# Counting a 388-column weight piece as 0.76 of a step in a schedule written out by hand

## The chip, the cores and the metric

The kernel runs on one core of a Trainium2 chip. The metric is the device time of one execution in microseconds; the median of three runs is compared. One execution is also profiled, and its trace is what the text reads.

## What is computed

Two layers, each on x of 256 x 2048 with one combined input projection that feeds three kinds of heads. The output of each kind is gated by a SiLU path, and one output projection and a normalisation follow. In short:

```python
h = x @ w_in
a_q, a_k, a_v, a_z, b_q, b_k, b_v, b_z, b_lr, m_q, m_z = jnp.split(h, cuts, axis=-1)
y_a = chunk_band_attention(heads_a(a_q), heads_a(a_k), heads_a(a_v), rel_table)   # 8 heads of 128
log_g = jax.nn.log_sigmoid(b_lr @ gate_w + gate_b) / GATE_TAU
o_b = gla_chunk_recurrence(heads_k(b_q), heads_k(b_k), b_v, heads_k(log_g))       # 4 heads
o_b = o_b * lax.rsqrt(jnp.mean(jnp.square(o_b), axis=-1, keepdims=True) + RMS_EPS) * gla_norm_g
y_m = memory_attention(heads_m(m_q), heads_m(mk), heads_m(mv))                    # 4 heads, 256 memory rows
y = jnp.concatenate([y_a * silu(a_z), y_b * silu(b_z), y_m * silu(m_z)], axis=-1)
x = layer_norm(DEEPNORM_ALPHA * x + y @ w_out, ln_g, ln_b)
```

## The kernel before

**Projections.** Every projection is a stream of weight pieces. `piece` (L128) loads one piece with a DMA on SP's queue and splits it into a high part (a cast on ScalarE, L116) and a low part (a subtraction on VectorE, L117), because the products are formed from split operands; the pool holds four raw pieces and four of each part. TensorE multiplies each piece with the resident x (all through `mm`, L93). There are two shapes of stream. `ws_group` (L254) runs two halves of four pieces with 256 columns and four rows of k each; a group is 8 pieces. `as_group` (L272) runs 8 pieces of `n` columns and two rows of k; `n` is 512 for the memory values, the GLA gate and the output projection, and 388 for the four value projections, `values(0)` to `values(3)` (L797).

**The order.** The order on TensorE and on SP's queue is the program's own (L49). VectorE and ScalarE are ordered by the scheduler when the program is built, with the splits of weights at a high priority; on the chip that order is then fixed. The work that isn't projection is written as Python generators: `gla` (L311), eight `a_head`s (L503), four `m_head`s (L537), `gla_turned` (L487), and in the second layer `transposed` (L574) and `restored` (L602). A generator issues a stretch of instructions, yields the number of ticks until its next stretch, and so on. `tick` (L52) is called after each weight piece: it raises `now` by one, keeps at most two generators active, and runs at most one stretch that is due (a generator that ends hands on to the next within the same tick). So a stretch is placed on TensorE's queue behind the piece whose tick ran it, and everything that it issues, its DMAs too, goes there. `finish` (L69) ticks on until named generators are done.

**The order of a layer** is: memory keys and values; GLA's q and k (BQK); `values(0)`, `values(1)`; then `gla` is put into the queue; for each half `values(2 + half)`, the queries (AQ) and the keys (AK), then four `a_head`s into the queue (L831 to L836); the memory queries (MQ), then four `m_head`s; the GLA gate (BZ), the other gates, and the output projection. Below, V0 to V3 are the value projections, and "V3 #2" is the second piece of V3.

**What the stretches hold.** `gla` has eight, with yields of 2, 6, 2, 6, 6, 3 and 2 ticks between them. Counted from 0: 0 and 1 are the gates' logits, their sigmoid and the running sum (table functions on ScalarE); 2 turns the decayed keys on TensorE; 3 to 5 hold the decayed products in six levels, each level a subtraction, |.|, an exponential and two products (L376), matmuls (L316) and a masked copy on VectorE (L335); 6 the outputs (L451 to L471), with four PSUM banks, four copies on ScalarE (L465) and eight squares (L470); and the end is an inverse square root (L285, with Sqrt on ScalarE, L289) and two scalings (L476). An `a_head` has three, with yields of 3 and 2 ticks between them and of 2 at its end: the bias load for the head two further on (L506) and the scores with their softmax (L508 to L521), the transposes (L526) with a copy (L528), and the values (L532, L534). `restored` multiplies and adds the normalisation's rows, two VectorE operations a stretch (L607, L608), eight stretches 2 ticks apart; it is put into the queue ahead of V0 in the second layer and finished (L827) ahead of V2.

The pool of PSUM banks that the stretches use has four (L84), taken in turn.

Of the kernel before, what the change touches and what calls it, by code (L numbers as in the profile page):

```python
# [36 lines left out]
def hybrid_trunk_kernel(  # L37
# [11 lines left out]
    ctx.enter_context(tc.manual_schedule(engines={PE, mybir.EngineType.SP}))  # L49
    waiting, active, done, now = [], [], set(), [0]  # L50

    def tick():  # L52

        now[0] += 1
        while True:
            while waiting and len(active) < 2:
                active.append((waiting.pop(0), 0))
            due = [e for e in active if e[1] <= now[0]]
            if not due:
                return  # L60
            active.remove(due[0])
            g = due[0][0]
            after = next(g, None)
            if after is not None:
                active.append((g, now[0] + after))
                return
            done.add(g)

    def finish(gens):  # L69
        while not all(g in done for g in gens):  # L70
            tick()
# [16 lines left out]
    def nm(s):  # L88
        uid[0] += 1
        return f"{s}_{uid[0]}"  # L90
# [28 lines left out]
    def load_quarter(src):  # L119

        with tc.high_priority(AHEAD):
            raw = wp.tile([P, 4, T], F32, name=nm("raw"), tag="raw")
            x = operand()
            sp.dma_start(raw, src)
            parts(x[0], x[1], raw)
        return x

    def piece(src, n, kp=2, home=None):  # L128

        with tc.high_priority(AHEAD):  # L130
            raw = wp.tile([P, kp, n], F32, name=nm("raw"), tag="raw")
            if home is None:
                hi, lo = (wp.tile([P, kp, n], F32R, name=nm(w), tag=w) for w in ("wh", "wl"))
            else:
                hi, lo = home
            if isinstance(src, list):
                w = n // len(src)
                for i, part in enumerate(src):
                    sp.dma_start(raw[:, :, i * w:(i + 1) * w], part.rearrange("p (k n) -> p k n", k=kp))
            else:  # L140
                sp.dma_start(raw.rearrange("p k n -> p (k n)"), src)
            parts(hi, lo, raw)
        return hi, lo
# [96 lines left out]
    def ws_half(src, xq):  # L240

        acc = psd.tile([P, 2, 2, T], F32, name=nm("acc"), tag="acc")
        for pc in range(4):
            wh, wl = piece(src[pc], 256, 4)
            xh, _, both = xq[pc]
            for j in range(4):
                for b in range(2):
                    mm(acc[:, b].rearrange("p h t -> p (h t)"), wh[:, j, b * P:(b + 1) * P], both[:, j], pc == j == 0, False)
                for b in range(2):
                    mm(acc[:, b, 1], wl[:, j, b * P:(b + 1) * P], xh[:, j], False, pc == j == 3)  # L250
            tick()
        return acc
# [11 lines left out]
    def as_products(o, t, xq, w, kt, kk, first=0):  # L264
        wh, wl = w
        xh, xl, _ = xq[kt // 4]
        j, ts = kt % 4, slice(t * P, (t + 1) * P)
        mm(o, xh[:, j, ts], wh[:, kk], kt == first, False)
        mm(o, xl[:, j, ts], wh[:, kk], False, False)
        mm(o, xh[:, j, ts], wl[:, kk], False, kt == 15)  # L270

    def as_group(src, xq, n, kp=2, first=None):  # L272

        acc = psd.tile([P, 2, 512], F32, name=nm("acc"), tag="acc")
        for pc in range(16 // kp):
            if first is not None and pc % 2 == 0:
                xq.append(load_quarter(first[pc // 2]))
            w = piece(src[pc], n, kp)
            for kk in range(kp):
                for t in range(2):  # L280
                    as_products(acc[:, t, :n], t, xq, w, pc * kp + kk, kk)
            tick()
        return acc

    def rsqrt(dst, src, n, epsc):  # L285
# [474 lines left out]
    for l in range(L):  # L760
# [3 lines left out]
        if l == 0:  # L764
            def each(p):
                if p in (2, 4, 6, 7):
                    xq.append(resident_quarter(len(xq), xT[len(xq)]))

            first_memory(mk, mv, each)
        else:  # L770
            memq = []
            parts(*mv, as_group(w512[l, G_MV], memq, 512, 2, memT))
            gens = [transposed(xq, gbT), restored(gb)]
            waiting.append(gens[0])
            for i, a, b in ws_group(w512[l, G_MK], memq):
                tmp = scratch([P, 2, T])
                total(tmp, a, b)
                parts(mk[0][:, i:i + 2], mk[1][:, i:i + 2], tmp)
            finish(gens[:1])
# [17 lines left out]
        def values(i):  # L797
            acc = as_group(w388[l, i], xq, 388)
            act.copy(asv[:, :, i * 388:(i + 1) * 388], acc[:, :, :388])
# [38 lines left out]
        for i, a, b in ws_group(w512[l, G_MQ], xq):  # L838
# [5 lines left out]


        acc = as_group([[w512[l, G_BZ, h * 4 + pc // 2][:, pc % 2 * 512:pc % 2 * 512 + 512] for h in range(2)]
                        for pc in range(8)], xq, 512)
        finish(gens[0])
# [156 lines left out]
```

## Time and profile before

| | us |
|---|---|
| median of 3 runs | 927.55 |
| lowest and highest | 927.30, 927.62 |
| span of the profiled execution | 924.8 |
| TensorE busy in it | 917.4 |
| VectorE busy | 588.4 |
| ScalarE busy | 497.1 |
| DMA, bytes moved | 178.85 MB, 193 GB/s in the mean |

The profile gives no time of its own for the profiled execution beside its span, which runs from the first to the last instruction. The median of the runs lies 2.75 us above it, and this difference is taken for what lies around the span.

How to read its rows: PE is TensorE's matmuls, PEld its weight loads, which run beside them, DVE VectorE, ACT ScalarE, SP the queue of DMAs. A row of the waits has the waiting engine, what it was to write and its line, what it waited for, then the sum in us, how often, and the longest. A row of the chain has its start, its length, and what ran. A row of the timeline has its start, length, engine, line, operation, the tile written and those read, shapes and count, and in brackets the idle time before it with what ended it. A row of the groups has the count, then busy us, mean ns of one, and the idle time before.

### The profile page before, as it was taken

The page shows a single profiled execution, that of the slowest core. Times are in us where ns is not written, and L with a number is a line of the kernel's source. Part 1 is how long each engine was busy: PE and PEld are TensorE (multiplying, and loading weights), DVE is VectorE, ACT ScalarE, POOL GpSimd, SP SyncE. Part 2 cuts the span into 40 slices and gives each one's busy share as a digit, 9 for nine tenths or more (in the row PEclk, how much of TensorE's full clock was granted, in tenths as well). Part 3 has the DMA queues.
Part 4 walks back from the last instruction along what each step waited for, and adds up shares of the span by engine and source line. Part 5 has one row for each costly group of instructions (what it writes and reads, how often), then busy time and mean ns, then how long its engine had stood idle before and what let it go on. Part 6 is the DMA issues. An engine that isn't in the chain of part 4 may idle for free.

```text
span 924.8 us, 14242 instructions
## 1 busy us (share of the span) xinstructions
PE 917.4 (99%) x5500; PEld 807.1 (87%) x5500; DVE 588.4 (64%) x812; ACT 497.1 (54%) x714; POOL 21.9 (2%) x49
## 2 busy tenths in 40 slices
PE   9999999999999999999999999999999999999997
PEld 8889998998888888888888899889888888888885
DVE  6764488564564666555587674975646555766565
ACT  6644475574454675433466446656544555754350
POOL 1000000000000000000000000000000000110000
PEclk9999999999999999999999999999999999999999
DMA  9956865555555566766675566565555544676652
GB/s 310 332 187 176 303 208 158 167 191 172 187 160 161 172 202 206 214 193 196 213 252 175 151 205 190 182 184 166 189 185 176 166 152 160 197 223 221 200 163 91
DMA packets 71253, 178.85 MB, mean 193 GB/s; under 512 B 7304, under 2 KB 31240, under 8 KB 70928
## 3 DMA queue, kind: packets, MB, share of 16 engines
q1 hardware_dynamic: 69120, 173.30, 58.4%
q0 software_dynamic: 1920, 4.36, 2.0%
q8 instruction: 43, 0.70, 0.3%
q10 hardware_dynamic: 144, 0.26, 0.1%
q14 instruction: 26, 0.21, 0.1%
HBM read 175.77 MB, written 2.10 MB: 192 GB/s over the span
## 4 chain that ended last, share of the span: by engine, by line
PE 95%; ACT 2%; issue 1%; DVE 1%; DMA 0%; SPq 0%; DVEq 0%; ACTq 0%
PE acc L93 86%; PE bk L93 7%; ACT wh L116 1%; PE bk L526 1%; ACT sc L470 1%; DMA raw<-w 0%; PE bk L561 0%; PE bk L590 0%; ACT L518 0%; ACT L289 0%; ACT yr L465 0%; PE bk L494 0%; DVE yr L476 0%; ACT sc L518 0%; ACT sc L528 0%
## 5 line engine op out<-in xcount | busy, mean ns | idle before, releaser
L117 DVE TENSOR_TENSOR wl<-raw,wh 128x1024 fp32r<-128x1024 f32 (+3 forms) x321 | 369.9, 1154 | 252.6 <-ACT wh L116 250.1
L116 ACT CAST wh<-raw 128x1024 fp32r<-128x1024 f32 (+3 forms) x321 | 318.4, 994 | 327.3 <-PE acc L93 229.7
L93 PE MATMUL acc<-x,wh 128*128 128x512 f32 x1248 | 397.6, 400 | 0.1
L93 PE MATMUL acc<-wh,x 128*128 128x512 f32 (+2 forms) x1236 | 358.1, 371 | 0.0
L93 PEld LDWEIGHTS acc<-x,wl 128*128 128x128 f32 x1248 | 234.4, 188 | 55.3
L93 PEld LDWEIGHTS acc<-wh,x 128*128 128x128 f32 x1236 | 227.5, 189 | 27.6 <-issue 0.3
L93 PE MATMUL acc<-x,wl 128*128 128x256 f32 x1248 | 246.0, 278 | 0.0
L93 PE MATMUL acc<-wl,x 128*128 128x512 f32 (+2 forms) x618 | 228.1, 369 | 0.0
L93 PEld LDWEIGHTS acc<-x,wh 128*128 128x128 f32 x1248 | 191.8, 189 | 1.8 <-ACT wh L116 0.3
L93 PEld LDWEIGHTS acc<-wl,x 128*128 128x128 f32 x618 | 116.2, 188 | 14.5 <-DVE wl L117 0.6
L518 ACT ACTIVATE sc<-sc,mx 128x128 f32<-128x128 f32 (+1 forms) x32 | 14.4, 449 | 21.8 <-DVE mx L516 21.8
L382 ACT ACTIVATE sc<-sc 128x512 f32<-128x512 f32 x12 | 7.6, 633 | 18.4 <-DVE sc L380 18.4
L511 DVE SCALAR_TENSOR_TENSOR sc<-bk,bias 128x384 f32<-128x384 f32 x16 | 8.9, 556 | 12.3 <-PE bk L93 12.2
L117 DVE TENSOR_TENSOR x<-sc,x 128x512 fp32r<-128x512 f32 x20 | 13.3, 684 | 0.7 <-ACT x L116 0.7
L116 ACT CAST x<-raw 128x1024 fp32r<-128x1024 f32 x5 | 5.3, 1052 | 15.0 <-DMA raw<-memT 12.6
L117 DVE TENSOR_TENSOR x<-raw,x 128x1024 fp32r<-128x1024 f32 x5 | 6.1, 1220 | 11.0 <-ACT x L116 11.0
L93 PE MATMUL bk<-qk,qk 128*128 128x128 f32 (+1 forms) x64 | 13.1, 326 | 0.0
L93 PE MATMUL bk<-sc,asv 128*128 128x256 f32 (+1 forms) x64 | 13.0, 326 | 0.0
L262 DVE SCALAR_TENSOR_TENSOR sc<-acc,sc 128x512 f32<-128x512 f32 x19 | 12.9, 681 | 0.0
L117 DVE TENSOR_TENSOR x<-res,x 128x512 fp32r<-128x512 f32 (+2 forms) x14 | 10.4, 764 | 3.9 <-ACT x L116 3.9
L623 DVE SCALAR_TENSOR_TENSOR res<-res,acc 128x512 f32<-128x512 f32 x15 | 9.7, 683 | 5.0 <-PE acc L93 5.0
L116 ACT CAST x<-sc 128x512 fp32r<-128x512 f32 x20 | 11.8, 615 | 1.3 <-DVE sc L598 1.3
(209 smaller groups left out, 568.4 us busy)
## 6 DMA issues: line engine op xcount, KB each, us to landing
raw<-w SPq DMA_DIRECT2D x214, 512.0 KB, 4.0
raw<-w SPq DMA_DIRECT2D x64, 388.0 KB, 3.4
raw<-w SPq DMA_DIRECT2D x83, 256.0 KB, 3.2
bias<-relw SPq DMA_DIRECT2D x16, 192.0 KB, 3.8
res<-xT SPq DMA_DIRECT2D x4, 512.0 KB, 4.9
res<-xn SPq DMA_DIRECT2D x1, 2048.0 KB, 8.2
raw<-memT SPq DMA_DIRECT2D x4, 512.0 KB, 4.2
res<-memT SPq DMA_DIRECT2D x6, 256.0 KB, 6.2
```

The costliest lines, as they stand in the source:

```text
L93: pe.matmul(o, l, r, start=start, stop=stop, skip_group_check=True)
L116: act.copy(hi, src)
L117: dve.tensor_tensor(lo, src, hi.bitcast(F32), op=ALU.subtract)
L262: dve.scalar_tensor_tensor(dst, a, scale, dst, op0=ALU.mult, op1=ALU.add)
L382: act.activation(dd, dd, AF.Abs)
L470: act.activation(sq, on[par][:, g], AF.Square, scale=1.0 / math.sqrt(P), accum_out=ms[:, par * 4 + g:par * 4 + g + 1])
L511: dve.scalar_tensor_tensor(s, pb[:, :384], SCALE, bias[h], op0=ALU.mult, op1=ALU.add)
L518: act.activation(s[:, own[t]], s[:, own[t]], AF.Exp, bias=mx[:, t:t + 1], accum_out=zs[:, t:t + 1])
L526: pe.transpose(pt[:, i * P:(i + 1) * P], s[:, i * P:(i + 1) * P], ident)
L623: dve.scalar_tensor_tensor(r, r, ALPHA, acc, op0=ALU.mult, op1=ALU.add)
```

## The change

`tick` takes a share, 1 unless given, and raises `now` by it. `as_group` passes its columns over 512. So a piece of 388 columns counts 388/512 = 0.7578; the pieces of 512 columns and those of `ws_group` count 1 as before. The yields stay as they are.

```diff
-    def tick():
+    def tick(share=1.0):
 
-        now[0] += 1
+        now[0] += share
...
             for kk in range(kp):
                 for t in range(2):
                     as_products(acc[:, t, :n], t, xq, w, pc * kp + kk, kk)
-            tick()
+            tick(n / 512)
         return acc
```

## The prediction

> **What bounds the kernel now.** I read the page first, then who TensorE's two queues wait for, then the stretches in which the moved steps lie, and last the order of work inside them.
>
> ```profile
> span 924.8 us, 14242 instructions
> PE 917.4 (99%) x5500; PEld 807.1 (87%) x5500; DVE 588.4 (64%) x812; ACT 497.1 (54%) x714; POOL 21.9 (2%) x49
> PEclk9999999999999999999999999999999999999999
> ```
>
> TensorE is busy for 917.4 of 924.8 us at full granted clock. A busy share alone can hide waits, so the next view asks for them: first the matmuls' waits, all of them, then the weight loads' waits that bear on this change.
>
> ```profile
> PE bk L93 <- DVE eps L759: 1.1, 1, 1.1
> PE bk L526 <- DVE sc L521: 0.5, 2, 0.3
> PE bk L93 <- ACT nparts L116: 0.3, 1, 0.3
> PE bk L734 <- DVE nt L696: 0.3, 1, 0.3
> ```
>
> ```profile
> PEld bk L526 <- DVE sc L521: 1.2, 2, 0.6
> PEld bk L93 <- DVE mx L516: 0.5, 2, 0.2
> ```
>
> The first row is the start of the program; the last two (tiles of the closing normalisation) are its end. Between them the matmuls wait in one place per layer: L526, the transposes of an attention head, for L521, the last operation of that head's softmax. It costs 0.5 us in all (0.27 each by the rows below). That is what the change can win; with the weight loads' waits at the same places the bound is 1.2 + 0.5 = 1.7 us.
>
> The place is found in the stretches by group of weight pieces. In order: the fourth value projection (V3) of layer 0, the query projection behind it (AQ1), the memory-query projection (MQ), and V3 of layer 1.
>
> ```profile
> 173.96:195.57 21.61, 21.34 (x168) 20.41 (x167) 14.12 (x29) 18.36 (x43) 1.62 (x4) 1.00 0.55 182
> 195.57:221.88 26.31, 26.31 (x154) 23.14 (x155) 15.06 (x23) 12.69 (x23) 0.00 (x0) 1.00 0.49 163
> 244.85:270.45 25.60, 25.60 (x152) 22.56 (x152) 14.82 (x23) 13.02 (x24) 0.00 (x0) 1.00 0.53 166
> 629.86:651.46 21.60, 21.33 (x168) 20.40 (x167) 13.98 (x29) 18.36 (x43) 0.00 (x0) 1.00 0.57 180
> ```
>
> The columns are length, then busy PE, weight loads, VectorE, ScalarE. V3 is where ScalarE is fullest, 18.36 of 21.61 us, and where TensorE misses 0.27; in AQ1 and MQ ScalarE has half its time free and TensorE misses nothing. So the bound is TensorE's own pace, and the one inner wait is ScalarE's crowd in V3.
>
> **The change, part by part.** Only pieces of 388 columns count differently, 388/512 = 0.758; the 512-column calls still count 1. In layer 0, V0 and V1 run with no generator waiting. What moves is found by following the yields through the ticks by hand (gla.n is the n-th stretch of the GLA generator between yields, from 0; ah is an attention head; #n the weight piece behind which it comes):
>
> - gla.1: V2 #3 to #4; gla.2: AQ0 #1 to #3; gla.3: AQ0 #3 to #5; gla.4: AK0 #1 to #3; gla.5: AK0 #7 to V3 #2
> - gla.6: V3 #2 to #6; gla's end (the rsqrt): V3 #5 to AQ1 #1
> - ah0.0 stays at V3 #1; ah0.1: #4 to #5; ah0.2: #6 to #8
> - ah1.0: V3 #5 to AQ1 #1; ah1.1: V3 #8 to AQ1 #4; ah1.2: AQ1 #2 to #6
> - ah2: AQ1 #1, #4, #6 to #2, #5, #7; ah3: AQ1 #5, #8, AK1 #2 to AQ1 #8, AK1 #3, #5
> - layer 1, restored: every second piece becomes every third, and its last two steps come together behind V1 #8
>
> From MQ on every step stands where it stood. No matmul, DMA, cast or activation is added or removed, so the sum holds only waits.
>
> *The wait removed.* The late link and what it waited for, TensorE first, then the chain that ended last, then ScalarE:
>
> ```profile
> 187.49 0.82 PE L93 MATMUL bk<-qk,qk 128*128 128x128 f32 x4
> 195.57 0.70 PE L526 MATMUL bk<-ident,sc 128*128 128x128 f32 x3 [0.27 <-DVE sc L521]
> ```
>
> ```profile
> 173.96 2.12 PE acc L93 x12
> 178.86 1.91 PE bk L93 x56
> 196.27 2.80 PE acc L93 x16
> ```
>
> ```profile
> 180.38 2.38 ACT L465 COPY yr<-bk 64x512 f32<-64x512 f32 x4 [0.22 <-PE bk L93]
> 186.49 0.48 ACT L528 COPY sc<-bk 128x384 f32<-128x384 f32 x1
> 189.10 1.28 ACT L289 ACT_TABLE_LOAD   x1
> 190.39 0.30 ACT L289 ACTIVATE rs_u<-ms,eps 128x8 f32<-128x8 f32 x1
> 191.65 1.28 ACT L518 ACT_TABLE_LOAD   x1
> 192.94 0.40 ACT L518 ACTIVATE sc<-sc,mx 128x128 f32<-128x128 f32 x1
> ```
>
> ah1's scores start at 187.49, its transposes at 195.57: 8.08 us, because its exponentials (192.94) stand behind gla.6's copies and the rsqrt with two table loads, 189.10 to 192.94 = 3.84 us. Three pieces of 2.12 us plus two small steps gave it only 7.8 us.
>
> After the change ah1.0 to ah1.1 spans three pieces of AQ1 with ah2.0 between. MQ already has exactly this pattern of pieces and steps (ah4.0 behind #1, ah5.0 behind #2, ah4.1 behind #4):
>
> ```profile
> 247.63 0.66 PE bk L93 x4
> 248.29 2.78 PE acc L93 x16
> 251.07 0.66 PE bk L93 x4
> 251.73 5.57 PE acc L93 x32
> ```
>
> ```profile
> 251.46 0.55 DVE L521 TENSOR_SCALAR sc<-sc,zs 128x128 f32<-128x128 f32 x2
> 256.77 0.55 DVE L521 TENSOR_SCALAR sc<-sc,zs 128x128 f32<-128x128 f32 x2
> ```
>
> The allowance is 0.66 + 2.78 + 0.66 + 5.57 = 9.67 us. In MQ the two softmaxes end at 252.01 and 257.32, 4.4 and 6.2 us after their scores. With the rsqrt block of 3.84 us in front, ah1 needs 4.4 + 3.84 = 8.2 us, close to the 8.08 measured; I take 8.2. It is 1.5 us early, so the wait of 0.27 goes in each layer: **-0.54 us**. What is next behind it is ah2, below.
>
> *ScalarE's load.* V3 loses the rsqrt block without its cast (2 x 1.28 + 0.30 = 2.86) and ah1's exponentials (about 1.3), and gains none, since gla.5 is TensorE and VectorE alone: about 14.2 us of 21 to 22. AQ1 goes to about 12.69 + 4.2 = 16.9 of 26.3. Each cast runs four buffers ahead of its matmuls, so nothing on the path.
>
> *gla.2 to gla.5.* The spacing in time is kept: six pieces stay six, and gla.4 to gla.5 goes from six long pieces (6 x 2.80 = 16.8) to five long and two short (18.2). Cost zero, hidden by the TensorE pieces between. Without that cover a step would cost what its chain is late; the trace shows no such wait.
>
> *PSUM banks and gla.6.* gla.6 takes all four, now one piece behind ah0.1, whose bank ScalarE's copy L528 must free. In the trace its transposes start at 185.04 and the copy ends at 186.97, 1.93 us later; one piece gives 2.12, and that bank is the last of the four to be written.
>
> ```profile
> 185.04 0.49 PE L526 MATMUL bk<-ident,sc 128*128 128x128 f32 x3
> ```
>
> Bound 0 to 0.2 us; I take 0. ah0.2 follows gla.6 by two pieces, as ah0.1 did.
>
> *restored.* Two steps of two VectorE operations each come together behind V1 #8.
>
> ```profile
> 527.00 0.69 DVE L607 TENSOR_TENSOR res<-res,gb 128x512 f32<-128x512 f32 x1
> 527.73 0.69 DVE L608 TENSOR_TENSOR res<-res,gb 128x512 f32<-128x512 f32 x1
> ```
>
> That is 4 x 0.69 = 2.8 us in front of V2's splits, which run up to four pieces (8.5 us) ahead: hidden, and at most 2.8 us once if they weren't. The extra ticks of that finish issue nothing on TensorE.
>
> *SP's queue.* ah3's load of a bias waits for ah1's scores to have been read, and weight DMAs queue behind it. It stood eight pieces behind them (V3 #5 to AQ1 #5), now seven (AQ1 #1 to #8).
>
> ```profile
> raw<-w SPq DMA_DIRECT2D x214, 512.0 KB, 4.0
> bias<-relw SPq DMA_DIRECT2D x16, 192.0 KB, 3.8
> ```
>
> If SP stands there until ah1.0 has been read, the next weights land 4.0 us after it, and seven pieces of 2.80 us = 19.6 us pass before they are used: hidden.
>
> The sum is 0 - 0.54 = -0.54 on the span: 924.8 to 924.3. The median of the runs shown, 927.55, lies 2.75 us above the span; I keep that difference: **927.0 us**. The bounds of the sum are -1.7 (every wait of V3's loads gone too) and +0.4 (0.2 per layer at the banks): 925.85 to 927.95.
>
> [...] The trace has the loads at 1.28 us each. [...]
>
> **The rivals.**
>
> *The square root falls between two heads (ah1 before it, ah2 behind it).* As a mechanism in rows: ah2's softmax takes 6.2 + 3.84 = 10.0 us, and its allowance from AQ1 #2 to #5 is about 0.66 + 5.57 + 0.3 + 2.80 = 9.3. TensorE waits 0.7 instead of 0.27, +0.9 in the two layers: 928.4. For it: the rsqrt becomes ready about when ah1's scores do. Against: the 6.2 contains queueing behind ah4 that would not be paid twice. [...]
>
> *Slower: the two heads stack up behind the rsqrt in AQ1.* ScalarE and VectorE keep a fixed order. The parts of a head there:
>
> ```profile
> L518 ACT ACTIVATE sc<-sc,mx 128x256 f32<-128x256 f32 x16 | 8.0, 497 | 0.0
> L518 ACT ACTIVATION_READ_ACCUMULATOR sc<-sc,mx 128x1 f32 x32 | 6.0, 186 | 0.0
> L511 DVE SCALAR_TENSOR_TENSOR sc<-bk,bias 128x384 f32<-128x384 f32 x16 | 8.9, 556 | 12.3 <-PE bk L93 12.2
> L516 DVE TENSOR_REDUCE mx<-sc 128x1 f32<-128x256 f32 x16 | 6.5, 409 | 0.0
> ```
>
> ```profile
> 247.44 1.05 ACT L116 CAST wh<-raw 128x1024 fp32r<-128x1024 f32 x1 [1.24 <-PE acc L93]
> ```
>
> If that order puts ah2's two exponentials with their read-outs (0.40 + 0.50 + 2 x 0.19 = 1.3 us), its scaling and two maxima (0.56 + at most 2 x 0.41, about 1.3) and one cast (1.05) ahead of ah1's end, ah1 takes 8.08 + 3.65 = 11.7 us against 9.67. TensorE then waits 2.06 at AQ1 #4, less 0.27: +1.8 in each layer, +3.6: **931.1**. It decides from a softmax longer than 9.67 us.
>
> Against it: in MQ, ah4 was finished (252.01) before ah5 was begun.
>
> *Nothing changes:* the wait only moves to another step: 927.5. For it: 0.27 us is small beside any reordering of ScalarE.
>
> *Faster by over 0.2%* needs 1.86 us, more than all inner waits together (1.7). It would take time hidden in the pace of the pieces, which the chain shows constant (2.12 and 2.80).
>
> **How the numbers follow.** The wait gone, 927.0: 0.58. Nothing changes or the square root between two heads, 927.5 to 928.4: 0.24. Slower by stacking or another late chain, 931.1: 0.14. Faster beyond the bound: 0.04. About 0.2%, 1.86 us, is what a measurement of this kernel can tell from no change; so faster 0.04, same 0.82, slower 0.14. The range starts at 925.9, the lower bound, and ends at 929.4, where slower begins, which leaves out 0.18.
>
> **What would show it.** Right: no idle time before L526 in either layer; ScalarE in V3 near 14 us and in AQ1 near 17; two table loads still, now beside AQ1 #1 to #2; the stretch up to V2 and all from MQ on unchanged. Wrong: idle time on TensorE before the transposes behind AQ1 #4 or #5, a wait of gla.6 for L528, a late cast early in V2 of layer 1, or more table loads than before.

## The result and the profile after

The changed kernel takes 925.91 us in the median of 20 runs, the kernel before 927.34 us in 20 runs of its own: ratio 0.9985, 95% interval 0.9979 to 0.9991. That is 1.4 us less (0.8 to 1.9), inside the 0.2% that was taken as what a measurement can tell; with twenty runs of each it is told from no change.

The first lines of the page after, in the order of those shown of before:

```profile
span 923.8 us, 14249 instructions
PE 916.7 (99%) x5500; PEld 806.5 (87%) x5500; DVE 587.9 (64%) x812; ACT 498.2 (54%) x714; POOL 21.8 (2%) x49
PEclk9999999999999999999999999999999999999999
```

The work is the same: 5500 matmuls, 812 instructions of VectorE, 714 of ScalarE. The matmuls' waits, all of them:

```profile
PE bk L93 <- DVE eps L759: 1.1, 1, 1.1
PE bk L93 <- ACT nparts L116: 0.3, 1, 0.3
PE bk L734 <- DVE nt L696: 0.3, 1, 0.3
```

The row of L526 is gone, and no other has come. Now V3 and AQ1 of layer 0 (length, then busy PE, weight loads, VectorE, ScalarE):

```profile
172.89:194.85 21.96, 21.96 (x228) 21.08 (x228) 13.18 (x21) 13.03 (x25) 1.53 (x4) 1.00 0.61 197
194.85:221.15 26.30, 26.30 (x155) 23.21 (x155) 15.27 (x28) 17.55 (x37) 0.00 (x0) 1.00 0.54 176
```

ScalarE fell from 18.36 to 13.03 us in V3 and rose from 12.69 to 17.55 in AQ1, where there is room. TensorE is busy in all of both.

To see where the time came from without what differs at the start of a run, I measure one stretch per layer on TensorE's queue: from GLA's first transposes (L340, behind V2 #1 in both kernels) to the first transposes of the gated result (L494, behind AZ0 #6 in both). Timeline of the kernel before, both layers:

```profile
108.24 0.38 PE L340 MATMUL bk<-ident,lr 128*128 128x128 f32 x2
316.08 0.60 PE L494 MATMUL bk<-ident,yr 128*128 128x128 f32 x4
...
564.11 0.38 PE L340 MATMUL bk<-ident,lr 128*128 128x128 f32 x2
771.99 0.60 PE L494 MATMUL bk<-ident,yr 128*128 128x128 f32 x4
```

And of the kernel after:

```profile
108.48 0.38 PE L340 MATMUL bk<-ident,lr 128*128 128x128 f32 x2
315.71 0.60 PE L494 MATMUL bk<-ident,yr 128*128 128x128 f32 x4
...
563.73 0.38 PE L340 MATMUL bk<-ident,lr 128*128 128x128 f32 x2
771.00 0.60 PE L494 MATMUL bk<-ident,yr 128*128 128x128 f32 x4
```

The stretch was 207.84 and 207.88 us and is 207.23 and 207.27: **0.61 us less in each layer**, 1.22 in all. Between the layers' stretches lie 248.03 and 248.02 us, so nothing changed there, the restored rows of layer 1 included. The start went 0.24 us the other way in this pair of executions. The spans differ by 1.0 us and the medians by 1.4, because the profiled execution of before was a fast one: every run on record lasts 1.7 to 1.9 us longer than its span, so of the 2.75 us between 927.55 and 924.8 about 1 us is a difference between executions and doesn't lie around the span.

But the idle time that went was 0.27 us per layer. The rest of the 0.61 stands in the length of the late step itself. In the chain of the kernel before, the three transposes took 0.70 us where TensorE had waited for them, and 0.33 us for the next head, where it had not:

```profile
195.57 0.70 PE bk L526 x3
...
208.74 0.33 PE bk L526 x3
```

In the chain of the kernel after, the same step of head 1 is an ordinary one:

```profile
207.32 0.33 PE bk L526 x3
```

So 0.27 + 0.37 = 0.64, close to the 0.61. The weight loads of head 1's transposes show part of it, before and after, with the matmul of after below them:

```profile
195.57 0.46 PEld L526 LDWEIGHTS bk<-ident,sc 128*128 128x128 f32 x3 [0.59 <-DVE sc L521]
207.05 0.35 PEld L526 LDWEIGHTS bk<-ident,sc 128*128 128x128 f32 x3
207.15 0.49 PE L526 MATMUL bk<-ident,sc 128*128 128x128 f32 x3
```

Before, the loads stood idle for 0.59 us and began with their matmuls at 195.57; after, they began 0.10 us ahead of them, beside the last matmul of the piece. The idle time of the matmuls counts from the end of the one before, and that end is modelled: it says 0.27.

### The profile page after: what moved, and what is told of

It reads as the page before. It is cut to its first block, busy times and chain, and to the rows that moved or that the text cites. A ratio compares the mean times of both kernels' runs of the same rounds, so it can differ in the third digit from the quotient of the medians.

```text
span 923.8 us, 14249 instructions
## 1 busy us (share of the span) xinstructions
PE 916.7 (99%) x5500; PEld 806.5 (87%) x5500; DVE 587.9 (64%) x812; ACT 498.2 (54%) x714; POOL 21.8 (2%) x49
## 4 chain that ended last, share of the span: by engine, by line
PE 98%; DMA 0%; DVE 0%; ACT 0%; SPq 0%; issue 0%
PE acc L93 89%; PE bk L93 8%; PE bk L526 1%; DMA raw<-w 0%; PE bk L561 0%; PE bk L590 0%; PE bk L494 0%; PE bk L393 0%; SPq L177 0%; ACT res L746 0%; ACT wh L116 0%; DVE stats L731 0%; PE bk L340 0%; DVE res L730 0%; DVE res L682 0%
## 5 line engine op out<-in xcount | busy, mean ns | idle before, releaser
L93 PE MATMUL acc<-x,wh 128*128 128x512 f32 x1248 | 398.0, 400 | 0.1
L93 PE MATMUL acc<-wh,x 128*128 128x512 f32 (+2 forms) x1236 | 357.3, 370 | 0.1
L93 PEld LDWEIGHTS acc<-x,wl 128*128 128x128 f32 x1248 | 234.4, 188 | 55.3
L93 PEld LDWEIGHTS acc<-wh,x 128*128 128x128 f32 x1236 | 227.0, 188 | 27.9 <-ACT wh L116 0.6
L93 PE MATMUL acc<-x,wl 128*128 128x256 f32 x1248 | 246.0, 278 | 0.0
L93 PE MATMUL acc<-wl,x 128*128 128x512 f32 (+2 forms) x618 | 228.0, 369 | 0.0
L93 PEld LDWEIGHTS acc<-x,wh 128*128 128x128 f32 x1248 | 192.0, 189 | 1.9 <-ACT wh L116 0.4
L93 PEld LDWEIGHTS acc<-wl,x 128*128 128x128 f32 x618 | 116.0, 188 | 15.0 <-DVE wl L117 0.9
L93 PE MATMUL bk<-qk,qk 128*128 128x128 f32 (+1 forms) x64 | 13.1, 326 | 0.0
L93 PE MATMUL bk<-sc,asv 128*128 128x256 f32 (+1 forms) x64 | 13.0, 326 | 0.0
L262 DVE SCALAR_TENSOR_TENSOR sc<-acc,sc 128x512 f32<-128x512 f32 x19 | 12.9, 681 | 0.0
```

What stands on the lines that cost most here:

```text
L93: pe.matmul(o, l, r, start=start, stop=stop, skip_group_check=True)
L262: dve.scalar_tensor_tensor(dst, a, scale, dst, op0=ALU.mult, op1=ALU.add)
```

## The experiments

Theory: all of the gain is head 1's wait, made by ScalarE's chain (gla.6's copies and squares, the inverse square root with two table loads, then head 1's exponentials). First rival: it comes from all steps being spaced out. The first four runs part them, the next four measure the loss against the wait, the last doubles the change.

The runs in one table; the stretch is that of layer 0 and layer 1, idle time that of the matmuls at L526.

| run | ratio to before | 95% interval | stretch, us | idle at L526, us |
|---|---|---|---|---|
| the change | 0.9985 | 0.9979 to 0.9991 | 207.23, 207.27 | 0, 0 |
| e1_only_v3 | 0.9986 | 0.9977 to 0.9995 | 207.24, 207.24 | 0, 0 |
| e2_not_v3 | 0.9997 | 0.9988 to 1.0006 | 207.69, 207.75 | 0, 0 |
| e3_ah1_late | 0.9988 | 0.9979 to 0.9997 | 207.24, 207.27 | 0, 0 |
| e4_no_sqrt | 0.9986 | 0.9977 to 0.9995 | 207.23, 207.25 | 0, 0 |
| e5_squares_before | 1.0077 | 1.0063 to 1.0091 | 212.14, 210.52 | 2.96, 2.95 |
| e6_squares_after | 0.9994 | 0.9985 to 1.0002 | 207.41, 207.49 | 0, 0 |
| e7_after_ah1_2 | 1.0024 | 1.0015 to 1.0034 | 207.56, 211.19 | 0, 2.00 |
| e8_after_ah1_1 | 1.0102 | 1.0088 to 1.0116 | 212.55, 212.57 | 3.48, 3.48 |
| e9_half | 1.0008 | 0.9999 to 1.0017 | (its ends move) | 0, 0 |

**e1_only_v3: only V3's pieces count 0.76.**

```diff
-            tick(n / 512)
+            tick(share)          # as_group's new argument
-            acc = as_group(w388[l, i], xq, 388)
+            acc = as_group(w388[l, i], xq, 388, share=388 / 512 if i == 3 else 1.0)
```

> Only V3's pieces count 0.76; V0 to V2 count 1, so every GLA stretch up to the fifth stands where it stood before. Theory (one chain): from the end of gla's outputs (gla.6) ScalarE's copies, squares, the inverse square root with its two table loads and head 1's exponentials take 14.8 us to the end of head 1's softmax (180.8 to 195.5 before, 189.8 to 204.7 after), and TensorE waits if it has less work than that between gla.6 and head 1's transposes: 14.3 us before, 17.4 after. Here it has about 17.7 (gla.6 behind V3 #3, the transposes behind AQ1 #2), so no wait: the whole gain, -1.3 us against before, and no idle time ahead of L526. Rival (spacing): the gain is from all stretches standing further apart in V0 to V3; then this keeps a quarter to a half of it, -0.3 to -0.6 us.

It took 925.93 us, 1.28 below before, and its stretch is the changed kernel's to 0.03 us. None of the moves in V0 to V2, AQ0 and AK0 is needed; the spacing rival falls.

**e2_not_v3: V0 to V2 count 0.76, V3 counts 1.**

```diff
-            acc = as_group(w388[l, i], xq, 388)
+            acc = as_group(w388[l, i], xq, 388, share=1.0 if i == 3 else 388 / 512)
```

> V0 to V2 count 0.76, V3's pieces count 1. Most of the moved stretches move as in the changed kernel, but gla.6 stands behind V3 #4 and head 1's transposes behind AQ1 #1. Theory (one chain): TensorE has about 12.8 us of work between them where the chain takes 14.8, so it waits about 2.0 us in each layer and takes 0.4 us more to come back, 2.4 against 0.64 before: +1.7 per layer, +3.5 us against before. Rival (spacing): the larger part of the gain stays, -0.6 to -1.0 us against before.

It took 926.86 us, within its interval of before, not 3.5 us more. The wait stayed, as the theory said against its rival, but small: the stretch shows a loss of 0.46 and 0.48 us against the changed kernel, where the kernel before has 0.61. The gain that the rival gave, 0.6 to 1.0 us, isn't there either. The step that failed was a fixed 14.8 us for ScalarE's chain. ScalarE's timeline there:

```profile
194.57 1.28 ACT L289 ACT_TABLE_LOAD   x1
195.87 0.30 ACT L289 ACTIVATE rs_u<-ms,eps 128x8 f32<-128x8 f32 x1
196.19 1.28 ACT L518 ACT_TABLE_LOAD   x1
197.48 0.40 ACT L518 ACTIVATE sc<-sc,mx 128x128 f32<-128x128 f32 x1
```

From the first load to the exponential it takes 2.91 us, where the kernel before had 3.84 with a cast between. And the end of the chain is on VectorE. In the kernel before, GLA's two scalings stand between the reciprocal of head 1's softmax and its last operation:

```profile
193.96 0.17 DVE L519 RECIPROCAL zs<-zs 128x2 f32<-128x2 f32 x1 [1.00 <-ACT sc L518]
194.05 1.27 DVE L476 TENSOR_TENSOR yr<-yr,rr 128x512 f32<-128x512 f32 x2
195.24 0.54 DVE L521 TENSOR_SCALAR sc<-sc,zs 128x128 f32<-128x128 f32 x2
```

Here they come behind it. The order of both engines is made anew for each program, so the chain was 13.4 us here (from the end of gla.6 near 185.7 to TensorE's transposes at 199.05) against 12.9 us of TensorE's work. No matmul counts as idle there at all, and yet the late transposes take their 0.70 us in the chain, their weight loads wait 0.34 us, and half a microsecond is lost.

**e3_ah1_late: the kernel before, with head 1's transposes one tick later.**

```diff
-        yield 3
+        yield 4 if h == 1 else 3       # the first yield of a_head
```

> The kernel before with one number changed: head 1's first yield is 4 instead of 3, so its transposes come behind AQ1 #1 instead of V3 #8; GLA and the restored rows stand as before. Theory (one chain): 17 us of TensorE's work against 14.8, no wait, the whole gain: -1.3 us against before, of which only 0.5 us was idle time of the matmuls and the rest is the way back after the wait (the chain's row for the three transposes 0.33 us as elsewhere, instead of 0.70). Rival (spacing): one step a piece later is worth no more than the idle time, -0.5 us, or nothing.

926.20 us, 1.0 below before, with a stretch of 207.24 and 207.27 us: one number changed in the kernel before gives the whole gain in the stretch. By the ticks this moves other steps of heads 1 to 3 too, each by one or two pieces, but none of GLA's and none of the restored rows. Its chain has the ordinary step:

```profile
199.72 0.33 PE bk L526 x3
```

So the loss per layer was 0.6 us and not the 0.27 of idle time.

**e4_no_sqrt: the kernel before without the two table loads.** Identity stands in for Sqrt in GLA's normalisation, so this part of the computation is changed.

```diff
-        act.activation(u, src, AF.Sqrt, bias=eps[:, epsc:epsc + 1])
+        act.activation(u, src, AF.Sqrt if epsc == 0 else AF.Identity, bias=eps[:, epsc:epsc + 1])
```

> The kernel before with Identity in place of Sqrt in GLA's normalisation (that part of the computation is changed), so that both table loads of 1.28 us beside it go; every step stands as before. Theory (one chain): the chain is 2.6 us shorter, 12.2 against 14.3 us of TensorE's work: no wait, -1.3 us against before at the old places of all steps. Rival (the place on TensorE's queue itself costs, not what it waits for): no change, within 0.3 us.

925.92 us, 1.29 below before, stretch 207.23 and 207.25, with every step on TensorE's queue at its old place. The place costs nothing; what it waits for does. With e3 this settles the cause: the same wait, removed from TensorE's side or from ScalarE's, is worth the whole change.

**e5_squares_before: the kernel before with four squares twice.**

```diff
-            for g in range(4):
+            for g in (0, 1, 2, 3) if par == 0 else (0, 0, 1, 1, 2, 2, 3, 3):
```

> The kernel before with four of gla.6's eight squares done twice (the same values again): ScalarE's chain ahead of head 1's exponentials is 4 x 0.435 = 1.74 us longer, every step on TensorE stands as before. Theory: TensorE's idle time ahead of L526 grows one for one, from 0.27 to 2.0 us in each layer, and the fixed part of the loss (0.34 us of the 0.61 per layer: the way back) stays: the stretch from GLA's first step to the turned gate goes from 207.84 to 209.6 us, +3.5 us for both layers. Rival (the loss is a cost of the place and only happens to stand beside a wait): +0 to +1 us. Rival (the chain has slack that the scheduler uses, as it seemed in the run in which V3 alone was not counted): clearly less than 3.5, about +1 to +2.

934.24 us, 7.1 above before: twice the forecast. Two things were missed. The idle time grew by 2.7 us, not 1.74. VectorE's timeline shows why:

```profile
196.37 0.16 DVE L519 RECIPROCAL zs<-zs 128x2 f32<-128x2 f32 x1
197.53 1.23 DVE L117 TENSOR_TENSOR wl<-raw,wh 128x1024 fp32r<-128x1024 f32 x1 [0.99 <-ACT wh L116]
198.67 0.54 DVE L521 TENSOR_SCALAR sc<-sc,zs 128x128 f32<-128x128 f32 x2
```

The fixed order has a split ahead of L521; it waits 0.99 us for its cast while head 1's softmax stands behind it, finished but for that one operation. From the reciprocal to L521 it takes 2.30 us here and took 1.28 in the kernel before: 1.74 + 1.02 = 2.76, the 2.7. And against an undisturbed 207.24 us the stretch lost 4.90 us in layer 0 for 2.96 of idle time, and 3.28 in layer 1 for 2.95. The stretches of layer 0 around the wait (clock in the third column from the right):

```profile
196.00:199.00 3.00, 0.05 (x1) 0.00 (x0) 2.00 (x5) 3.00 (x6) 0.00 (x0) 1.00 0.56 175
199.00:202.40 3.40, 3.40 (x14) 2.83 (x15) 1.34 (x2) 0.62 (x2) 0.00 (x0) 0.71 0.69 173
202.40:206.00 3.60, 3.60 (x20) 3.18 (x19) 1.25 (x2) 1.05 (x1) 0.00 (x0) 0.80 0.34 132
206.00:210.00 4.00, 4.00 (x25) 3.50 (x25) 2.90 (x7) 2.19 (x6) 0.00 (x0) 1.00 0.43 131
```

Behind the wait the granted clock is 0.71 and 0.80: 3.40 x 0.29 + 3.60 x 0.20 = 1.7 us lost, an estimate from the two rows. So 4.90 = 2.96 + 1.7 + 0.2. In layer 1 the clock stayed at 1.00, and 3.28 = 2.95 + 0.33, close to the 0.34 that the theory had beside the idle time.

**e6_squares_after: the same squares in the changed kernel.**

> The changed kernel with the same 1.74 us of additional squares. Theory: head 1's softmax ends 2.5 us ahead of its transposes there (204.7 against 207.15), so the 1.74 us are hidden: no idle time ahead of L526, within 0.3 us of the changed kernel, -1.2 against before. Rival (the room is used up by what is crowded into AQ1 now): a new wait of 0.5 us or more at L526 or before a cast.

926.46 us, 0.7 below before. The additional 1.74 us cost 0.18 and 0.22 us per layer, nine tenths of them hidden. In layer 0 head 1 is not late; head 2's transposes are, by their length (0.61 against 0.49):

```profile
207.05 0.49 PE L526 MATMUL bk<-ident,sc 128*128 128x128 f32 x3
210.26 0.61 PE L526 MATMUL bk<-ident,sc 128*128 128x128 f32 x3
```

In layer 1 it is head 1 itself: its transposes start at 662.57 and take 0.70 us, because VectorE has head 2's scaling, a split and head 2's maxima ahead of its last operation. So the room is used up there.

**e7_after_ah1_2 and e8_after_ah1_1: the changed kernel with head 1's transposes one and two ticks earlier.**

```diff
-        yield 3
+        yield 2 if h == 1 else 3       # 1 in e8
```

> The changed kernel with head 1's first yield at 2 instead of 3: its transposes come behind AQ1 #3, 6.9 us of TensorE's work behind its scores, where its softmax takes 7.2. Theory: a wait about as short as that of before, idle time 0.1 to 0.4 us, and a loss of that plus 0.34 us in each layer: the stretch 207.7 to 208.0 us, so the gain of the change is lost again (within 0.4 us of before). Rival (the loss is the idle time alone): 0.2 us per layer less than that, -0.7 against before.

> The same with head 1's first yield at 1: its transposes come behind AQ1 #2, 3.4 us of TensorE's work behind its scores. Theory: TensorE waits 3.8 us less what the order of ScalarE gives back, and 0.34 us for the way back: +4.1 us in each layer against the changed kernel, +7.0 against before, at most; the fixed part is read from the rows as the loss of the stretch less the idle time and should again be 0.3 to 0.4 us. Rival (the way back grows with the wait): the difference between loss and idle time is above 0.6 us.

e7 took 929.48 us, 2.3 above before, because its two layers differ. In layer 0 the loss was 0.33 us against the changed kernel's stretch, without the 0.1 to 0.4 us of idle time that was expected with it. In layer 1 the transposes waited:

```profile
661.77 0.90 PE L526 MATMUL bk<-ident,sc 128*128 128x128 f32 x3 [2.00 <-DVE sc L521]
```

There VectorE has head 2's scaling, a split and head 2's maxima ahead of head 1's last two operations, so the softmax took 9.2 us and not 7.2. The loss was 3.9 us: 2.0 idle, 1.7 of clock (rows below), and 0.2. e8 took 936.63 us, 9.5 above before, where 7.0 was the most that was expected: 5.3 us lost in each layer. In layer 0 3.5 of them are idle, 1.7 of clock (rows below), 0.1 beyond both; in layer 1, of whose clock no row is shown, 3.5 are idle and 1.8 stand beside them. So what is lost beyond idle time and clock doesn't grow with the wait (0.1 to 0.35 us in e5 to e8, and 0.46 to 0.48 in e2, which has no idle time), but it isn't one fixed amount; and a second loss comes in one step, with the clock: 1.7 us behind waits of 2.00, 2.96 and 3.48 us alike, and none behind one of 2.95. Neither theory had that.

**e9_half: a piece of 388 columns counts 0.38.**

```diff
-            acc = as_group(w388[l, i], xq, 388)
+            acc = as_group(w388[l, i], xq, 388, share=388 / 1024)
```

> The change in twice its size and more: a piece of 388 columns counts 0.38. GLA's outputs come behind AQ1 #4, head 1's transposes behind AK1 #1, the heads run on into the gates, and five of the eight steps of the restored rows come in one lump behind V1 #8 (ten operations of VectorE, 6.9 us). Theory: with the one wait gone nothing is left to win inside, so this is at the changed kernel's time, within 0.4 us of it and -1.2 us against before, unless the lump outlasts the four pieces (8.5 us) that the splits run ahead, which would show as a wait of TensorE for a split early in V2 of layer 1 alone. Rival (more room goes on paying): -2 us or more against before.

928.06 us, not told from before, and not the 1.2 us less that was expected. The lump of restored rows made no wait, and L526 none; a new one came, in the chain ahead of the turned, gated result:

```profile
PE bk L494 <- DVE yr L485: 1.9, 2, 0.9
```

```profile
296.24 1.28 ACT L483
297.54 0.61 ACT sc L483
298.17 0.70 DVE yr L485
299.00 0.63 PE bk L494 x4
```

The heads now run on into the gates and leave a slot free earlier, so the turned result is due at AZ0 #1, right behind its gate's SiLU with a table load, where before it stood behind AZ0 #6. More room in one place took it from another. No run here has a stretch below 207.23 us, which the change reaches, and there no matmul waits any more; that no other placing could win is not shown.

## Why the prediction was right, and what it mis-sized

- **What bounds the kernel** held: TensorE's pace, with one inner wait per layer at L526. The steps moved as counted, and that wait went.
- **The size failed.** The step is "-0.54 us", two times the idle time of 0.27. The stretch gave 1.22 and the runs 1.4 (0.8 to 1.9). The price of a wait was taken as the idle time that the profile prints; it was that plus 0.34 us of way back, as e3 and e4 show from both sides. The weight loads' 0.59 us ahead of each L526 was nearly the loss itself.
- **The range held by luck in part.** Its lower end, 925.9, comes from the bound of 1.7 us, and 925.91 was measured. The first term of the bound, 1.2 us at L526, is what the stretch gave. The second, 0.5 us at L93 for L516, wasn't won: e3 and e4 still have that wait and the whole gain. Besides, the kernel before took 927.34 us in twenty runs and 927.55 in the first three, 0.2 more.
- **"I take 8.2"** for head 1's softmax: layer 0 has 7.2 (scores at 197.49, end at 204.69), because no cast stands in the rsqrt block. The need of 8.08 us was put down to ScalarE alone; 1.27 us of it were GLA's scalings on VectorE (L476, above). In layer 0 after:

```profile
198.94 1.28 ACT L289 ACT_TABLE_LOAD   x1
200.24 0.30 ACT L289 ACTIVATE rs_u<-ms,eps 128x8 f32<-128x8 f32 x1
200.56 1.28 ACT L518 ACT_TABLE_LOAD   x1
201.85 0.40 ACT L518 ACTIVATE sc<-sc,mx 128x128 f32<-128x128 f32 x1
```

- **The rival of two heads stacking up** was nearer than its 0.14 in one layer. In layer 1 of the changed kernel VectorE does take head 2's scaling (658.35) ahead of head 1's end:

```profile
658.35 0.55 DVE L511 SCALAR_TENSOR_TENSOR sc<-bk,bias 128x384 f32<-128x384 f32 x1
661.27 0.15 DVE L519 RECIPROCAL zs<-zs 128x2 f32<-128x2 f32 x1
661.46 0.55 DVE L521 TENSOR_SCALAR sc<-sc,zs 128x128 f32<-128x128 f32 x2
```

  Head 1 ends at 662.01 there, 9.2 us after its scores (652.78), with its transposes at 662.44: 0.4 us to spare against 2.5 in layer 0. e7 took 2.8 us of the allowance away and the rival became true in that layer. Its price of 1.8 us per layer left out the clock: a wait of 2.00 us, about the 2.06 that it gave, cost 3.9.
- **The square root between two heads** did not happen: in both layers head 1's exponentials follow both loads. The block is 2.91 us in layer 0 (198.94 to 201.85, rows above), with two loads of 1.28 us; in layer 1 two copies and a cast stand between its loads, of 1.28 us each too.
- **ScalarE's load** was put at about 14.2 and 16.9 us and is 13.03 and 17.55. **Banks, restored rows, SP's queue**: put at zero, and no wait of TensorE shows any. Of the restored rows three steps come together behind V1 #8, not two (554.92 to 560.5 on VectorE), since its own tick runs one and two more follow without a piece between.

## What to carry to other kernels

Where one engine's order is written out by hand and it is full, look for the few steps at which it waits, and price each by how much longer the whole stretch is than an undisturbed one, not by the idle time that the profile prints: here 0.6 us stood behind 0.27, and in one run half a microsecond behind none. A schedule rule that moves some forty steps may owe all its gain to one of them; move that one alone before believing the rule. Slack is to be read layer by layer, since the order of the other engines is made anew for each: the same code had 2.5 us to spare in one layer and 0.4 in the other.

## What the runs showed of the hardware

Behind three waits of TensorE the granted clock fell, and that cost another 1.7 us each time: in layer 0 of e5 (a wait of 2.96 us, with 0.71 and 0.80 in the rows shown with that run), in layer 1 of e7 (2.00 us, over at 661.77) and in layer 0 of e8 (3.48 us, over at 205.17). Two rows each of e7 and e8:

```profile
660.50:664.00 3.50, 2.23 (x8) 1.91 (x9) 2.92 (x9) 2.30 (x6) 0.00 (x0) 0.73 0.49 179
664.00:668.00 4.00, 4.00 (x20) 3.40 (x20) 0.62 (x3) 1.32 (x2) 0.00 (x0) 0.81 0.42 131
205.17:208.60 3.43, 3.43 (x15) 2.90 (x16) 1.25 (x2) 0.48 (x1) 0.00 (x0) 0.68 0.30 90
208.60:212.00 3.40, 3.40 (x18) 2.99 (x18) 1.18 (x2) 1.05 (x1) 0.00 (x0) 0.82 0.17 70
```

By the same estimate as in e5 that is 3.50 x 0.27 + 4.00 x 0.19 = 1.7 us in e7 and 3.43 x 0.32 + 3.40 x 0.18 = 1.7 us in e8. In e8 the rows on both sides (201.00 to 205.17 and 212.00 to 216.00) have 1.00. The matmuls show it too. Rows of e8 from the late transposes on:

```profile
205.17 0.61 PE L526 MATMUL bk<-ident,sc 128*128 128x128 f32 x3 [3.48 <-DVE sc L521]
205.54 0.71 PE L93 MATMUL acc<-x,wh 128*128 128x512 f32 x2
206.09 0.40 PE L93 MATMUL acc<-x,wl 128*128 128x256 f32 x2
206.32 0.97 PE L93 MATMUL acc<-x,wh 128*128 128x512 f32 x2
...
207.52 1.05 PE L93 MATMUL acc<-x,wh 128*128 128x512 f32 x2
208.37 0.63 PE L93 MATMUL acc<-x,wl 128*128 128x256 f32 x2
208.80 1.05 PE L93 MATMUL acc<-x,wh 128*128 128x512 f32 x2
...
211.31 0.62 PE L93 MATMUL acc<-x,wh 128*128 128x512 f32 x2
211.78 0.40 PE L93 MATMUL acc<-x,wl 128*128 128x256 f32 x2
212.01 0.63 PE L93 MATMUL acc<-x,wh 128*128 128x512 f32 x2
```

From one product with the high part to the next it is 1.28 us (207.52 to 208.80), and 0.70 us further on (211.31 to 212.01). The matmuls don't grow longer with the end of the wait: the first long row of them starts 1.15 us behind it here (206.32), and 1.24 us behind it in e5:

```profile
200.24 0.89 PE L93 MATMUL acc<-x,wh 128*128 128x512 f32 x2
```

Not every such wait brought it on. The other wait of e5, in layer 1, was 2.95 us long and ended at 659.16, and the clock stayed at 1.00:

```profile
658.00:661.00 3.00, 1.84 (x11) 1.54 (x12) 2.50 (x4) 1.78 (x3) 0.00 (x0) 1.00 0.35 90
661.00:664.00 3.00, 3.00 (x20) 2.69 (x19) 0.65 (x2) 1.05 (x1) 0.00 (x0) 1.00 0.82 276
664.00:668.00 4.00, 4.00 (x25) 3.50 (x25) 3.05 (x7) 2.19 (x6) 0.00 (x0) 1.00 0.42 133
```

What decides between the two isn't shown by these runs; the length of the wait alone doesn't, since 2.00 us brought the drop in e7 and 2.95 us didn't here. Of layer 1 of e8 only the mean of the whole run speaks: its profiled execution had a granted clock of 0.994, that of the kernel before 0.998, and 0.004 x 935 = 3.7 us, an estimate that the rounding leaves open by about 1 us, is near two times 1.7. From run to run e7's mean clock was 0.995 to 0.999, and its nine runs spread over 2.3 us; the changed kernel's twenty had 0.997 to 0.999 and spread over 1.4.
